# Hybrid mLSTM/MLA trunk: spilled feed-forward operands on ScalarE's DMA queue, loaded two chunks sooner; residuals a chunk later; context values in two parts

## The chip, the cores and the metric

One core of one Trainium2 chip runs the kernel. The metric is device microseconds (us) of one execution, the median over runs. TensorE (PE) multiplies, VectorE (DVE) and ScalarE (ACT) prepare and evacuate, GpSimd (POOL) and SyncE (SP) mostly issue DMAs; ACT can issue DMAs too.

## The reference, cut to what matters

Two layers over 256 latent and 256 context tokens of width 1024. Layer 0 mixes tokens with a chunked mLSTM, layer 1 with multi-head latent attention (MLA); each is followed by a gated convolutional feed-forward. The modulation rows ("ada") are a linear map of a condition vector.

```python
def _conv_ffn(h, w_in, conv_w, conv_b, w_out):
    gate, up = jnp.split(h @ w_in, 2, axis=-1)
    return (jax.nn.silu(_dwconv(gate, conv_w, conv_b)) * up) @ w_out
...
    m = jax.nn.silu(cond) @ w + b                       # _modulation: six parts per layer
...
    x = _layer_norm(ALPHA * x + ml[2] * yl, ln_g[i, 0], ln_b[i, 0])
    f = _conv_ffn(_modulate(x, ml[3], ml[4]), ffn_w_in[i], ffn_conv_w[i], ffn_conv_b[i], ffn_w_out[i])
    x = _layer_norm(ALPHA * x + ml[5] * f, ln_g[i, 1], ln_b[i, 1])
...
    kv = (_rms_norm(ckv, kv_norm) @ w_ukv).reshape(B, T, A_HEADS, A_DNOPE + A_DV)   # _mla_kv
    k_nope, v = jnp.split(kv, [A_DNOPE], axis=-1)
```

Context and latent tokens go through the same weights. All of it is float32 in and out.

## The kernel before, in words

**Products.** Every float32 product is three matmuls: each operand is split into a high and a low part, and `mm3` (L383 to L385) adds high by high, high by low and low by high. An operand's split is a copy on ACT and a subtraction on DVE; for weights that is L323 and L326.

**Weights.** `Stream` holds one list of weight pieces of 128x1024, in the order in which they are used. Its loads go out on SP's queue (L281), into a ring of raw buffers that depends on the stage; a load waits until the buffer's last split has ended. At most three split pieces (`w`, NB = 3) stand ready; pieces called wide go to other buffers (`wu`).

**Order.** Tile's planner places instructions on each engine's queue, mostly in the order in which the program names them. `keep_in_program_order` (`pin` in the code) fixes an instruction behind everything named before it on its engine. Background work is written as generators: `tick` runs a step of `bg` after each weight piece, and `n2` or an ADA number runs steps of `bg2`, which is the modulation (a step is one multiply-and-sum of 128x1024 on DVE, L512, and its rows come by SP's queue, L535). `ADA_M` is steps per piece of the mLSTM's output product, `ADA_F` steps per piece of the first feed-forward's input product.

**The feed-forward output of layer 0** (`w_fout0`) is a Strassen-like product of seven parts. The first four, in 24 chunks (`yt2`, `y11`, `yt3`, `yt1`, six of each), use operands that stay on the chip. The other three parts (`y21`, `y22`, `yt4`, six chunks each) use the operands named "2", "S4" and "3", which `act_sums` spilled to memory (`fd`, L1341 and L1347). `operand()` brings them back: it loads one (`zr`, L1367, one or two DMAs of 128 KB), and splits the one that was asked for two calls earlier (`fz`, L1373 on ACT, L1374 on DVE). There are 18 such operands. It is called at the chunks 10 to 23 and in the chunks of `y21` and `y22`. After chunk 23 the four products are copied out and added up (L1421 to L1433); then `residual()` forms the residual in eight background steps (L1441, L1442), and `add` puts the last products in (L1451 to L1453). The weights of `yt4` (and of its mLSTM sister `vt4`) are a sum: SP loads a piece that ACT spilled earlier (`raw<-t2d`, L278), and then POOL's queue adds the weights from memory into it (L279).

**After it** `mid` normalizes the context tokens, `mla_ctx` makes their compressed keys (`dkv`), `ukn(0)` the context keys (`kn`) and `uv(0)` the context values (`v`), while `tick`s run the latent tokens' normalization and transposes (`z_norm`, `ln_T`, L1199) in the background.

Of the kernel before, what the change touches and what calls it, by code (L numbers as in the profile page):

```python
# [38 lines left out]

VE = {1: (3, 0), 2: (3, 0), 3: (3, 0)}  # L40

ADA_U, ADA_T, ADA_Q, ADA_M, ADA_F = 1.4, 1.3, 1.6, 0.8, 1.05

# [309 lines left out]
class K:  # L355
# [996 lines left out]
    def w_fout0(self, x1d, mid):  # L1352


        nc, st, A = self.nc, self.st, self.fa
        pin = self.tc.keep_in_program_order
        parts = [("2", i) for i in range(6)] + [("S4", i) for i in range(6)] + [("3", i) for i in range(6)]
        off = {"2": 0, "3": 256, "S4": 512}
        got = []

        def operand():
            if parts:
                x, i = parts.pop(0)
                r = self.s2("zr")
                js = [j for j in (2 * i, 2 * i + 1) if j < 11]
                for h, j in enumerate(js):
                    pin(nc.gpsimd.dma_start(r[:, h * 256:(h + 1) * 256], self.fd[j][:, off[x]:off[x] + 256]))  # L1367
                got.append((x, js, r))
            if len(got) > 2 or not parts and got:
                x, js, r = got.pop(0)  # L1370
                n = 256 * len(js)
                u = self.u("fz")
                pin(nc.scalar.copy(u[:, 0, :n], r[:, :n]))  # L1373
                nc.vector.tensor_sub(u[:, 1, :n], r[:, :n], u[:, 0, :n])  # L1374
                for h, j in enumerate(js):
                    A[x, j] = u[:, :, h * 256:(h + 1) * 256]

        def prod(ps, x, w, i, bs=(0, 1)):
            for h in range(2 if i < 5 else 1):
                j = 2 * i + h  # L1380
                a = A[x, j]
                for b in bs:
                    ts = slice(b * 128, (b + 1) * 128)
                    cs = slice(h * 512, (h + 1) * 512)
                    self.mm3(ps[b], (a[:, 0, ts], a[:, 1, ts]), (w[0][:, cs], w[1][:, cs]), j == 0, j == 10)

        def pair():
            return [self.ps("y") for _ in range(2)]

        lo, hi = slice(0, 512), slice(512, 1024)  # L1390
        p6, p1, p7, p5 = [pair() for _ in range(4)]
        n = 0
        for i in range(6):
            for name, ps, x in (("yt2", p6, "S2"), ("y11", p1, "1"), ("yt3", p7, "S3"), ("yt1", p5, "S1")):
                w = st.use((name, 0, i))
                prod(ps, x, w, i)
                for f in ("S2", "1", "S3", "S1"):
                    if f == x:
                        for j in (2 * i, 2 * i + 1):
                            A.pop((f, j), None)  # L1400
                self.tick(1)
                if n >= 10:
                    operand()
                if n == 14:
                    gate = []
                    for g in (1, 0):
                        t = self.uf("gate")
                        nc.gpsimd.dma_start(t, self.gd[0, 5][g:g + 1, :].to_broadcast([128, 1024]))
                        gate.append(t)
                if n >= 16 and n % 2 == 0:  # L1410
                    if n == 16:
                        z = []
                    t = self.uf("z")
                    nc.gpsimd.dma_start(t, x1d[len(z)])
                    z.append(t)
                n += 1
        stats = [self.tiny(12, "st").rearrange("p (a b) -> p a b", b=6) for _ in range(4)]
        u1, u3, u4, vv = [], [], [], []
        for b in range(2):
            u = self.s2("u1")  # L1420
            nc.scalar.copy(u, p1[b])  # L1421
            u1.append(u)
            u = self.s2("u2")
            nc.vector.tensor_tensor(u, p6[b], u1[b], op=ALU.add)
            u4.append(u)
        for b in range(2):
            u = self.s2("u3")
            nc.vector.tensor_tensor(u, p7[b], u4[b], op=ALU.add)
            u3.append(u)
        for b in range(2):  # L1430
            v = self.s2("v")
            nc.vector.tensor_tensor(v, p5[b], u3[b], op=ALU.subtract)
            nc.vector.tensor_tensor(u4[b], p5[b], u4[b], op=ALU.subtract)  # L1433
            vv.append(v)

        def residual():

            for us, g, c in ((u1, 0, lo), (u4, 0, hi), (u3, 1, lo), (vv, 1, hi)):
                for b in range(2):
                    zz = z[2 * g + b]  # L1440
                    nc.vector.tensor_tensor(us[b], us[b], gate[g][:, c], op=ALU.mult)  # L1441
                    nc.vector.scalar_tensor_tensor(zz[:, c], zz[:, c], ALPHA, us[b], op0=ALU.mult, op1=ALU.add)  # L1442
                    if us is vv:
                        nc.vector.bn_stats(stats[2 * g + b][:, 1], zz[:, c])
                    yield

        def add(g, c, ps):
            for b in range(2):
                t = self.s2("zp")
                zz = z[2 * g + b][:, c]  # L1450
                nc.vector.tensor_tensor(t, ps[b], gate[g][:, c], op=ALU.mult)  # L1451
                nc.vector.tensor_tensor(zz, zz, t, op=ALU.add)
                nc.vector.bn_stats(stats[2 * g + b][:, c.start // 512], zz)  # L1453

        self.bg.append(residual())
        ps = pair()
        for i in range(6):
            w = st.use(("y21", 0, i))
            prod(ps, "2", w, i)
            self.tick(1)  # L1460
            operand()
        add(0, lo, ps)
        ps = pair()
        for i in range(6):
            w = st.use(("y22", 0, i))
            prod(ps, "S4", w, i)
            self.tick(1)
            operand()
        self.drain()
        add(0, hi, ps)  # L1470
        self.bg = [mid(0, z[0:2], stats[0:2])]
        self.step(self.bg)
        ps = pair()
        for i in range(6 - YTAIL):
            w = st.use(("yt4", 0, i))
            prod(ps, "3", w, i)
            self.tick(2)
        self.drain()
        mid(None, None, None)
        ws = [(i, st.use(("yt4", 0, i), hold=True)) for i in range(6 - YTAIL, 6)]  # L1480
        for b in range(2):
            for i, w in ws:
                prod(ps, "3", w, i, (b,))
        st.unhold("yt4")
        self.fa = self.fd = None
        self.bg = [mid(1, z[2:4], stats[2:4], lambda: add(1, lo, ps))]
# [94 lines left out]
            u = self.kn[h]  # L1581
            self.split(u[:, 0, cs], u[:, 1, cs], ps[:, hs])

    def uv(self, g):
        for t in (2 * g, 2 * g + 1):
            ts = slice(t * 128, (t + 1) * 128)
            for h in range(2):
                ps = self.ps("v1")
                c = slice(h * 512, (h + 1) * 512)
                for k in range(2):  # L1590
                    self.mm3(ps, (self.ckT[k][:, 0, ts], self.ckT[k][:, 1, ts]),
                             (self.wv[k][0][:, c], self.wv[k][1][:, c]), k == 0, k == 1)
                u = self.u("v1")
                self.split(u[:, 0], u[:, 1], ps)
                self.v1.append(u)
# [23 lines left out]
    def mla(self, hl):  # L1619
        nc, st = self.nc, self.st  # L1620
# [6 lines left out]
        for c in range(4):  # L1627
            w = st.use(("dq", 0, c))
            self.tick()
            for kk in range(2):  # L1630
                k = 2 * c + kk
                hi, lo = hl(k)
                cs = slice(kk * 384, (kk + 1) * 384)
                for t in range(2):
                    ts = slice(t * 128, (t + 1) * 128)
                    self.mm3(pss[t][:, :384], (hi[:, ts], lo[:, ts]), (w[0][:, cs], w[1][:, cs]), k == 0, k == 7)
        cq = []
        for t in range(2):
            r = self.s2("cq")
# [4 lines left out]
        g = self.smc("qng")  # L1644
# [11 lines left out]
        for c in range(2):  # L1656
            w = st.use(("uqr", 0, c))
            for kk in range(2 - c):
                k = 2 * c + kk
                cs = slice(kk * 512, (kk + 1) * 512)  # L1660
                for t in range(2):
                    ts = slice(t * 128, (t + 1) * 128)
                    self.mm3(pss[t], (cqT[k][:, 0, ts], cqT[k][:, 1, ts]), (w[0][:, cs], w[1][:, cs]),
                             k == 0, k == 2)
        self.drain()
        self.uv(1)
        self.ckT = self.wk = self.wv = None
        kn, v = self.kn, self.v1
        scale = float((DN + DR) ** -0.5)
# [2 lines left out]
        for t in range(2):  # L1672
            r = self.s2("qr")
# [111 lines left out]
def build(tc, off, a, out):  # L1785
    es = ExitStack()
    with es:
        k = K(tc, es, off, a)
        nc = k.nc
# [115 lines left out]
        st.pump(kv0 + PC)  # L1905
        k.mla_kv()
        k.ukn(0)
        k.tick(4)
        k.uv(0)
        k.drain()  # L1910
        k.take_late()
        att = k.mla(hl)
# [56 lines left out]
```

## Time and profile before

| what | value |
|---|---|
| median of 3 runs | 1399.56 us (1398.95 to 1405.11) |
| the profiled execution, its own time | 1403.48 us |
| its span, first to last instruction | 1401.7 us |
| mean granted TensorE clock | 0.992 |
| DMA queues, share of the 16 engines' span | SP's 48.1%, POOL's 13.9%, ACT's 3.0% |

The stages that the change touches: the mLSTM's output product ends at about 700 us of the span, the first feed-forward's input product runs from 720 to 946 us, `w_fout0`'s 24 chunks from 946 to 1007 us, `y21`, `y22` and `yt4` follow, and the context keys and values come from 1078 to 1097 us. Idle time of an engine is shown with the instruction after it and with what released that one. A window row gives, for each engine, busy us and the number of instructions, and then the granted clock, the DMA share and GB/s.

### The profile page before, as it was taken

The numbers are of one execution on the slowest core, as the hardware profiler recorded it, in microseconds if no ns is written. First come the engines' busy times: TensorE is split into PE (matmuls) and PEld (weight loads), VectorE is DVE, ScalarE is ACT, GpSimd is POOL, SyncE is SP. The second block draws the span as 40 slices with busy tenths as digits, with TensorE's granted clock in tenths as the row PEclk, the third lists the DMA queues.
The fourth block names the chain that finished last, engine by engine and source line by source line (L and its number), as shares of the span: only waits on it lengthen the run. The fifth ranks groups of instructions, "written<-read, shape, count | busy, mean of one in ns | idle before, by whom it ended". The sixth has DMA issues, their size and how long they took to land.

```text
span 1401.7 us, 19170 instructions
## 1 busy us (share of the span) xinstructions
PE 1359.0 (97%) x6903; PEld 1142.3 (81%) x6903; DVE 1074.7 (77%) x1726; ACT 699.5 (50%) x1179; POOL 139.0 (10%) x248
## 2 busy tenths in 40 slices
PE   6999999999999999999999999999968999999997
PEld 3788888888788888878798888888757988899986
DVE  6598756687688697699789777758878889776773
ACT  6585444435544545375543433434527667455560
POOL 0032000011011001110011000004111001000000
PEclk9999999999999999999999999999989999999999
DMA  9689847788675374667838667648767425367750
GB/s 336 222 293 321 282 163 240 244 293 283 203 226 194 102 243 152 210 214 229 255 134 289 221 224 213 213 146 292 263 174 223 148 83 202 122 190 229 206 189 30
DMA packets 94735, 297.63 MB, mean 212 GB/s; under 512 B 12136, under 2 KB 20584, under 8 KB 94640
## 3 DMA queue, kind: packets, MB, share of 16 engines
q1 hardware_dynamic: 68672, 218.52, 48.1%
q0 software_dynamic: 19056, 61.90, 13.9%
q10 hardware_dynamic: 6912, 15.99, 3.0%
q8 instruction: 54, 0.88, 0.2%
q14 instruction: 41, 0.34, 0.1%
HBM read 262.90 MB, written 33.46 MB: 211 GB/s over the span
## 4 chain that ended last, share of the span: by engine, by line
PE 44%; DVE 4%; DMA 3%; ACT 1%; issue 1%; POOL 0%; DVEq 0%; ACTq 0%; POOLq 0%; SPq 0%
PE fin L383 9%; PE fin L384 9%; PE fin L385 9%; PE y L384 4%; PE y L385 4%; PE y L383 4%; DMA raw<-in_ws 2%; DVE w L326 1%; DVE wu L326 1%; DMA zr<-fd 1%; PE s L1721 0%; DMA raw<-t2d 0%; PE dkv L383 0%; PE dkv L385 0%; PE dkv L384 0%
## 5 line engine op out<-in xcount | busy, mean ns | idle before, releaser
L326 DVE TENSOR_TENSOR w<-raw,w 128x1024 fp32r<-128x1024 f32 (+3 forms) x290 | 348.2, 1203 | 165.7 <-ACT w L323 165.0
L323 ACT CAST w<-raw 128x1024 fp32r<-128x1024 f32 (+3 forms) x290 | 300.4, 1037 | 331.1 <-PE fin L385 89.2
L384 PE MATMUL fin<-h,w 128*128 128x256 f32 (+1 forms) x696 | 231.7, 333 | 0.0
L385 PE MATMUL fin<-h,w 128*128 128x256 f32 (+1 forms) x696 | 231.4, 333 | 0.0
L383 PE MATMUL fin<-h,w 128*128 128x256 f32 (+1 forms) x696 | 231.2, 333 | 0.1
L512 DVE SCALAR_TENSOR_TENSOR junk<-ar,bc 128x1024 f32<-128x1024 f32 x128 | 155.8, 1217 | 3.6 <-ACT bc L554 1.7
L384 PEld LDWEIGHTS fin<-h,w 128*128 128x128 f32 x696 | 132.2, 190 | 13.1 <-DVE h L1212 0.2
L385 PEld LDWEIGHTS fin<-h,w 128*128 128x128 f32 x696 | 132.2, 190 | 12.7
L383 PEld LDWEIGHTS fin<-h,w 128*128 128x128 f32 x696 | 131.9, 190 | 13.1 <-ACT h L1211 0.3
L383 PE MATMUL qk<-xc,w 128*128 128x512 f32 x256 | 100.7, 393 | 0.0
L385 PE MATMUL qk<-xc,w 128*128 128x512 f32 x256 | 99.9, 390 | 0.0
L384 PE MATMUL qk<-xc,w 128*128 128x512 f32 x256 | 99.8, 390 | 0.0
L383 PEld LDWEIGHTS qk<-xc,w 128*128 128x128 f32 x256 | 48.1, 188 | 10.1 <-issue 0.4
L385 PEld LDWEIGHTS qk<-xc,w 128*128 128x128 f32 x256 | 48.1, 188 | 10.0
L384 PEld LDWEIGHTS qk<-xc,w 128*128 128x128 f32 x256 | 48.1, 188 | 9.6
L383 PE MATMUL up<-hT,w 128*128 128x512 f32 x128 | 50.5, 394 | 0.5 <-ACT hT L388 0.5
L384 PE MATMUL up<-hT,w 128*128 128x512 f32 x128 | 50.1, 392 | 0.5 <-DVE hT L389 0.5
L385 PE MATMUL up<-hT,w 128*128 128x512 f32 x128 | 50.1, 391 | 0.3 <-DVE w L389 0.3
L383 PE MATMUL tok<-w,hT 128*128 128x512 f32 x128 | 49.8, 389 | 0.0
L384 PE MATMUL tok<-w,hT 128*128 128x512 f32 x128 | 49.8, 389 | 0.0
L385 PE MATMUL tok<-w,hT 128*128 128x512 f32 x128 | 49.8, 389 | 0.0
L675 ACT ACTIVATE fg<-fg 128x512 f32<-128x512 f32 (+1 forms) x44 | 23.0, 523 | 53.6 <-DVE fg L673 48.0
(454 smaller groups left out, 3075.6 us busy)
## 6 DMA issues: line engine op xcount, KB each, us to landing
raw<-in_ws SPq DMA_DIRECT2D x287, 512.0 KB, 4.2
ar<-in_adaT SPq DMA_DIRECT2D x80, 512.0 KB, 4.4
adaw<-in_ada_w SPq DMA_DIRECT2D x32, 256.0 KB, 6.6
t2d<-raw ACTq DMA_DIRECT2D x13, 512.0 KB, 5.7
raw<-t2d SPq DMA_DIRECT2D x13, 512.0 KB
raw<-in_ws POOLq DMA_DIRECT2D x13, 512.0 KB, 7.7
zr<-fd POOLq DMA_DIRECT2D x33, 128.0 KB, 6.0
xmd<-xr POOLq DMA_DIRECT2D x16, 256.0 KB, 4.8
```

The source lines that it names most:

```text
L323: k.nc.scalar.copy(h[:, :cols], src)
L326: k.nc.vector.tensor_sub(l[:, :cols], src, h[:, :cols])
L383: mm(out, w[0], x[0], start=start, stop=False)
L384: mm(out, w[0], x[1], start=False, stop=False)
L385: mm(out, w[1], x[0], start=False, stop=stop)
L512: nc.vector.scalar_tensor_tensor(o, w, 1.0, self.bc[j], op0=ALU.mult, op1=ALU.mult, accum_out=col[:, k, j:j + 1])
L675: nc.scalar.activation(tmp[:, :n], tmp[:, :n], AF.Silu)
```

## The change: where operands are loaded, when, and what is paced

- `operand()` loads `zr` with `nc.scalar.dma_start` where it had `nc.gpsimd.dma_start`; it stays pinned, now on ACT.
- `operand()` is called from chunk 8 on, where it was chunk 10.
- `residual()` joins the background after the second chunk of `y21`, before its `tick`, where it joined ahead of the first.
- `uv` takes a list of token tiles; context tile 0's values are named ahead of `tick(4)`, tile 1's behind it.
- `ADA_M` goes from 0.8 to 0.6 and `ADA_F` from 1.05 to 1.25.

```diff
-ADA_U, ADA_T, ADA_Q, ADA_M, ADA_F = 1.4, 1.3, 1.6, 0.8, 1.05
+ADA_U, ADA_T, ADA_Q, ADA_M, ADA_F = 1.4, 1.3, 1.6, 0.6, 1.25
...
-                    pin(nc.gpsimd.dma_start(r[:, h * 256:(h + 1) * 256], self.fd[j][:, off[x]:off[x] + 256]))
+                    pin(nc.scalar.dma_start(r[:, h * 256:(h + 1) * 256], self.fd[j][:, off[x]:off[x] + 256]))
...
-                if n >= 10:
+                if n >= 8:
                     operand()
...
-        self.bg.append(residual())
         ps = pair()
         for i in range(6):
             w = st.use(("y21", 0, i))
             prod(ps, "2", w, i)
+            if i == 1:
+                self.bg.append(residual())
             self.tick(1)
             operand()
...
-    def uv(self, g):
-        for t in (2 * g, 2 * g + 1):
+    def uv(self, ts):
+        for t in ts:
...
-        self.uv(1)
+        self.uv((2, 3))
...
         k.ukn(0)
+        k.uv((0,))
         k.tick(4)
-        k.uv(0)
+        k.uv((1,))
         k.drain()
```

## The prediction, made before the change was run

> **What bounds the kernel now.** I read the page's busy times first, then windows of 5 us, then the chain of waits, then each engine's instructions in order of time at the one wide hole.
>
> ```profile
> PE 1359.0 (97%) x6903; PEld 1142.3 (81%) x6903; DVE 1074.7 (77%) x1726; ACT 699.5 (50%) x1179; POOL 139.0 (10%) x248
> ```
>
> TensorE is busy for 1359.0 of 1401.7 us, so all its waits together are 42.7 us, and a change that removes no matmul can win only from those. One hole is a quarter of them (columns: stretch, its us, busy us of PE, PEld, DVE, ACT, POOL with instructions, granted clock, DMA share, GB/s):
>
> ```profile
> 1030.00:1035.00 5.00, 1.05 (x5) 0.54 (x3) 0.00 (x0) 0.00 (x0) 0.31 (x1) 0.95 1.01 262
> 1035.00:1040.00 5.00, 0.00 (x0) 0.00 (x0) 3.27 (x6) 1.87 (x3) 0.88 (x1) 0.50 0.80 143
> ```
>
> From 1030 to 1035 us PE, DVE and ACT all stand while the DMA engines are full. The chain of waits (start, us, what) says for whom:
>
> ```profile
> 1019.93 5.27 DMA raw<-t2d
> ...
> 1025.77 0.90 POOL raw L279
> 1026.67 0.23 POOL zr L1367
> 1026.90 9.11 DMA zr<-fd
> ...
> 1040.15 1.14 DVE w L326
> ```
>
> POOL's adding DMA (L279) waits for a spilled weight; the last three operand loads stand behind it on POOL's queue, go out at 1026.7 and take 9.11 us. ACT's half of the operand's split waits for them, DVE's half for ACT's, and the weight split that PE wants stands behind that in DVE's order:
>
> ```profile
> 1036.73 1.03 DVE L1374 TENSOR_TENSOR fz<-zr,fz 128x512 fp32r<-128x512 f32 x2 [7.34 <-ACT fz L1373]
> ```
>
> ```profile
> 1041.34 0.80 PE L384 MATMUL y<-w,fz 128*128 128x512 f32 x1 [10.29 <-DVE w L326]
> ...
> 1043.64 0.63 PE L384 MATMUL y<-w,fz 128*128 128x512 f32 x1
> 1044.07 0.63 PE L385 MATMUL y<-w,fz 128*128 128x512 f32 x1
> ...
> 1045.09 0.39 PE L385 MATMUL y<-w,fz 128*128 128x512 f32 x1
> 1045.31 0.39 PE L383 MATMUL y<-w,fz 128*128 128x512 f32 x1
> ```
>
> The operands waited for are "3", used only in `yt4`, after the six pieces of `y22`: the order of the queues makes this stall, not need. PE starts the third piece of `y22` 10.29 us late, and then runs at a step of 0.43 instead of 0.22 us up to about 1044.9, some 1.5 us more.
>
> **The change part by part.**
>
> *The wait removed.* Calls from chunk 8 on issue 16 of the 18 loads ahead of `y21`; the last split is named in `y21`'s fourth piece, and no load stands behind L279 any more. DVE's 7.34 us of idleness goes. But DVE is full ahead of the hole:
>
> ```profile
> 1014.53 0.69 DVE L1374 TENSOR_TENSOR fz<-zr,fz 128x512 fp32r<-128x512 f32 x1
> 1015.14 0.69 DVE L1442 SCALAR_TENSOR_TENSOR z<-z,u 128x512 f32<-128x512 f32 x1
> 1015.74 1.22 DVE L326 TENSOR_TENSOR w<-raw,w 128x1024 fp32r<-128x1024 f32 x1
> ```
>
> ```profile
> 1007.07 0.50 PE L383 MATMUL y<-w,fz 128*128 128x512 f32 x1 [0.68 <-ACT u L1421]
> ...
> 1017.02 0.50 PE L384 MATMUL y<-w,fz 128*128 128x512 f32 x1 [1.02 <-DVE w L326]
> ```
>
> Instructions of 512 columns follow each other every 0.6 us, and at 1017.02 PE waited for DVE alone. Two operand splits move out of this stretch into the 24 chunks ahead: 2 x 0.6 = 1.2 us. One residual step (L1441 and L1442, 1.2 us) comes behind the split of `y22`'s third piece instead of ahead of it. That piece is ready 7.34 + 1.2 + 1.2 = 9.7 us earlier, at 1031.6; PE had run dry at 1041.34 - 10.29 = 1031.05, so about 1 us of waiting stays: DVE is late next. The late step is given back within `y22`, so DVE's last split there gains 7.34 + 1.2 = 8.5; PE's slow matmuls, 1.5 us, lay behind that and mostly go. Together 10.0 us. Bounds: 7.3, DVE's hole alone, and 12.8, all of 10.29 + 1.02 + 1.5.
>
> Does the short rest that stays slow the clock? These did:
>
> ```profile
> 690.79 0.50 PE L384 MATMUL y<-wu,hn 128*128 128x512 f32 x1 [0.57 <-DVE wu L326]
> ...
> 692.20 0.49 PE L383 MATMUL y<-wu,hn 128*128 128x512 f32 x1 [0.68 <-ACT wu L323]
> ...
> 693.45 0.80 PE L384 MATMUL y<-wu,hn 128*128 128x512 f32 x1 [0.76 <-DVE wu L326]
> 694.04 0.63 PE L385 MATMUL y<-wu,hn 128*128 128x512 f32 x1
> ```
>
> 2.0 us in three pieces, and a slow matmul of 0.63 us behind them; the one 1.02 us at 1017.02 had 0.50 and no more. I count nothing, bound 1.5. The Trainium skill, "TensorE: Matmul & The Clock Gate", Part 1 on the HAM clock gate, lets the half clock come after an idle window of some 3.4 us. By that a rest of 1 us costs nothing, and the sum stays; by the row at 693.45 it could be 1.5 us worse, since there 2.0 us were enough.
>
> *The new wait.* 33 DMA issues leave POOL's queue for ACT's. The mLSTM already does this with loads of its own:
>
> ```profile
> raw<-in_ws POOLq DMA_DIRECT2D x13, 512.0 KB, 7.7
> zr<-fd POOLq DMA_DIRECT2D x33, 128.0 KB, 6.0
> ...
> xcr<-xcd ACTq DMA_DIRECT2D x16, 256.0 KB, 8.4
> ```
>
> ```profile
> 331.62 0.85 ACTq L711 DMA_DIRECT2D xcr<-xcd  x2
> ...
> 339.29 0.62 ACT L716 CAST xc<-xcr 128x512 fp32r<-128x512 f32 x1 [1.17 <-DMA xcr<-xcd]
> ```
>
> ```profile
> DMA to landing us min/median/max: 2.2/6.0/10.1
> ```
>
> (KB each, median us to landing; then ACT in time; then the landing of `zr` on POOL.) Two issues take 0.85 us of ACT's queue. ACT rests longer than that per chunk:
>
> ```profile
> 992.83 1.06 ACT L323 CAST w<-raw 128x1024 fp32r<-128x1024 f32 x1 [1.10 <-PE y L385]
> ...
> 1000.99 0.62 ACT L323 CAST w<-raw 128x512 fp32r<-128x512 f32 x1 [1.52 <-PE y L385]
> ...
> 1004.67 0.61 ACT L1373 CAST fz<-zr 128x512 fp32r<-128x512 f32 x1
> ```
>
> What counts is landing. POOL ran far ahead of use; pinned on ACT, a load has its split two calls later. A chunk is 12 matmuls of 0.22, 2.7 us; two of them and one weight copy make 6.4 us, and the rest of 1.10 makes 7.5, under which a landing is hidden. The last four chunks are half as long: a load issued at 1000.99 has its split where 1004.67 stands, 3.7 us on. Behind that split on ACT are `y21`'s weight copies and the copies L1421, for which PE waits already at 1007.07. With the median of 6.0 they come 2.3 us late, with 2.2 not at all, with 10.1 6.4 us. I take 1.5 lost: nearest the median, less something for POOL's own queueing. The Trainium skill, "DMA: Bandwidth & Descriptors", section on issuing engines not being separate DMA queues, speaks against more: whoever issues, the same 16 engines carry it and only issue time is saved. By that the landing stays as it was and 2.3 is lost; the 9.11 us above agrees as far as a full DMA goes, but 1000 to 1010 us is not that stretch.
>
> *`yt4`'s weights.* PE comes 10 us earlier; do their sums?
>
> ```profile
> 1036.41 0.88 POOL L279 DMA_DIRECT2D raw<-in_ws  x1 [6.10 <-issue]
> ```
>
> ```profile
> 1051.63 0.69 DVE L1451 TENSOR_TENSOR zp<-y,gate 128x512 f32<-128x512 f32 x1 [1.05 <-PE y L385]
> ```
>
> The third lands at 1036.4 + 7.7 = 1044.1 if nothing moves it and is split 2.3 us later, at 1046.4; PE ended `y22` at 1051.6, so it wants that piece at 1051.6 - 10 + 2 x 2.7 = 1047. Hidden by 0.6 us; a landing of 10.1 costs 1.8. The later three wait for buffers that come free 8 to 10 us earlier. I take 0.5 lost, between 0 and 2.
>
> *Pacing.* 22 pieces carry `ADA_M`: 22 x 0.2 = 4.4 steps of L512 leave the mLSTM's output product for the feed-forward.
>
> ```profile
> L512 DVE SCALAR_TENSOR_TENSOR junk<-ar,bc 128x1024 f32<-128x1024 f32 x128 | 155.8, 1217 | 3.6 <-ACT bc L554 1.7
> ```
>
> ```profile
> 660.00:670.00 10.00, 10.00 (x49) 8.10 (x48) 10.00 (x20) 5.48 (x10) 0.55 (x1) 1.00 0.69 198
> 730.00:760.00 30.00, 30.00 (x134) 24.85 (x133) 29.23 (x49) 12.58 (x22) 6.51 (x12) 1.00 0.88 298
> ```
>
> That is 4.4 x 1.217 = 5.4 us of DVE, which is full at 660 to 670; its late weight splits free the buffers late, and the waits at 690 to 693 (2.0 us, then 1.4 us of slow matmuls) follow. Gain 0 to 3.4; I take 1.5. In the feed-forward PE never waits between 730 and 760, though DVE is at 29.23 of 30; 0.2 steps in each 5.4 us are 1.3 us more there, and two split pieces stand ready against it. Cost 0, up to 1.3 if they do not cover.
>
> *Context values in two parts.* Tile 0's 12 matmuls, 2.7 us, are named ahead of the transposes at which PE rests:
>
> ```profile
> 1083.72 0.78 PE L1199 MATMUL zT<-ident,z 128*128 128x128 f32 x4 [1.75 <-issue]
> 1085.27 0.39 PE L383 MATMUL kn<-ckT,wu 128*128 128x256 f32 x1 [0.77 <-DVE kn L389]
> ```
>
> ```profile
> 1083.66 1.16 DVE L326 TENSOR_TENSOR wu<-raw,wu 128x1024 fp32r<-128x1024 f32 x1
> ```
>
> But the second half of their weights is split only at 1084.8, so they fill little of 1.75 + 0.77 = 2.5 us, and could hold the transposes up by 1. I take 0.7 gained, from -1 to 2.5.
>
> **The sum.** 10.0 - 1.5 - 0.5 + 1.5 - 0 + 0.7 = 10.2 us. The profiled execution took 1403.48 us and would take 1393.3; it lies 3.9 above the median of the runs, which goes from 1399.56 to 1389.4.
>
> **The rivals.** *DVE and the sums keep half of it.* If the landing at the end of the chunks is 10.1 (6.4 lost instead of 1.5) or the slow clock and late sums cost 1.5 + 1.8, 4 to 5 us go: about 1394.5. For it speaks that DVE is full on both sides of the hole; against it that the hole itself is idle on every engine.
>
> *ACT becomes the bound: slower.* The load three calls on is named behind the split of this one, so three chunks can't be shorter than one landing and a split of 0.6 us. At 2.7 us a chunk this binds from a landing of 7.6 us; with 10.1 the chunk is 3.57 us, and 16 calls lose 14 us, which eats the gain: 1403. Slower by 0.5% needs 10.8 us; with 11.2, 19 us are lost, 1409. For it: `xcr` took 8.4 us on ACT's queue. Against: that wait at 339.29 was one of 1.17 us in 16 loads.
>
> *The change doesn't do what it says.* The planner could leave an unrelated wait in the same place on DVE, for instance ACT on `yt4`'s first sum: 1399.6.
>
> **How the numbers follow.** About 0.5% (7 us) is what a measurement of this kernel can tell from no change. Forecast, with its own range of 1386 to 1392.5: 0.56. Half of it, 1392.6 to 1398: 0.22. No change: 0.07. ACT's bound: 0.10, of which 0.03 ends within 0.5%. Better than 1386, where the upper bounds of pacing and values both come: 0.05. Faster by 0.5% is 0.56 + 0.05 = 0.61, the same 0.22 + 0.07 + 0.03 = 0.32, slower 0.07. The range leaves out ACT's bound and most of no change and of the better one: 1385 to 1398.5.
>
> **What would show it.** Right: no `zr` on POOL, no wait of DVE's L1374 near 7 us, PE's longest wait in `y22` under 2.5 us, `yt4` some 10 us earlier; fewer waits at 690; less rest at 1084. Wrong: ACT's L1373 waiting for `zr` by more than 2 us again and again, L1421 late, or ACT's L323 waiting for `yt4`'s sums.

## The result, and the profile after

The changed kernel takes 1388.92 us in the median of 4 runs (1388.60 to 1389.13), beside 1400.90 us (1398.95 to 1405.11, 4 runs) of the kernel before on the same chip: a ratio of 0.9910, 95% interval 0.9886 to 0.9935. Run again later it took 1387.91 us, 0.9904 (0.9890 to 0.9919). So it is faster, and about 12 us go. Its profiled execution took 1389.13 us with a span of 1387.4 us, 14.3 us under the profiled one of before; that one was among the slower of its kernel.

The page's busy line says that TensorE still does the same work:

```profile
PE 1355.8 (98%) x6903; PEld 1140.1 (82%) x6903; DVE 1075.0 (77%) x1726; ACT 699.2 (50%) x1179; POOL 121.2 (9%) x215
```

POOL issues 33 instructions fewer (215 for 248). The windows of 5 us in which the hole lay (columns as before) now look so; the same chunks come some 10 us earlier, so the window behind is shown too:

```profile
1025.00:1030.00 5.00, 3.65 (x17) 2.68 (x16) 5.00 (x8) 1.05 (x1) 0.38 (x2) 1.00 1.04 256
1030.00:1035.00 5.00, 5.00 (x24) 4.14 (x23) 5.00 (x8) 1.67 (x2) 0.83 (x1) 1.00 0.91 221
1035.00:1040.00 5.00, 5.00 (x24) 4.14 (x23) 5.00 (x8) 2.14 (x3) 0.00 (x0) 1.00 0.96 285
```

The DMA engines are as full as before, but VectorE no longer stands for them. It is busy for 5.00 of 5 us in each window: that is who is late next. TensorE's waits (line waited for: us in total, times, longest) and its rests in time:

```profile
PE y L384 <- DVE w L326: 3.2, 3, 1.3
...
PE y L383 <- ACT u L1421: 2.0, 1, 2.0
...
PE dkv L383 <- ACT hl L1211: 1.5, 1, 1.5
```

```profile
690.55 0.50 PE L384 MATMUL y<-wu,hn 128*128 128x512 f32 x1 [0.76 <-DVE wu L326]
...
1004.00 0.50 PE L383 MATMUL y<-w,fz 128*128 128x512 f32 x1 [2.04 <-ACT u L1421]
...
1010.89 0.50 PE L384 MATMUL y<-w,fz 128*128 128x512 f32 x1 [0.77 <-DVE w L326]
...
1027.72 0.50 PE L384 MATMUL y<-w,fz 128*128 128x512 f32 x1 [1.35 <-DVE w L326]
```

The row at 1027.72 is the third piece of `y22`, for which TensorE waited 10.29 us before. The one at 690.55 is all that is left of the three rests before 694. The loads, on the page:

```profile
zr<-fd ACTq DMA_DIRECT2D x33, 128.0 KB, 3.2
```

The 3.2 us there covers only 13 of the 33 loads, those whose landings the view could match. Read for every load from the events of its own semaphore in the trace, the landing takes 2.0 to 6.1 us, 4.0 in the median. For the kernel before, the view covers all 33: 2.2 to 10.1, and 6.0.

The first matmul of each stage, in each profiled execution, tells where the time went (us; "fin" is the first feed-forward's input product, "keys" the first matmul of `dkv`). The input product starts at 703.7 us in the kernel before, not at 720:

| kernel | start of fin | fin to `y21` | `y21` to keys | keys to end of span |
|---|---|---|---|---|
| before | 703.7 | 303.4 | 56.4 | 338.2 |
| changed | 699.3 | 304.7 | 44.6 | 338.8 |
| changed, run again | 698.0 | 304.6 | 44.7 | 338.9 |

So 4.4 us come ahead of the feed-forward, 1.3 are lost ahead of `y21`, 11.8 come from `y21` to `yt4`, and 0.6 are lost behind: 14.3 together.

### The profile page after: what moved, and what is told of

The parts are those of the page before. It is cut to its first block, busy times and chain, and to the rows that moved or that the text cites. A ratio compares the mean times of both kernels' runs of the same rounds, so it can differ in the third digit from the quotient of the medians.

```text
span 1387.4 us, 19172 instructions
## 1 busy us (share of the span) xinstructions
PE 1355.8 (98%) x6903; PEld 1140.1 (82%) x6903; DVE 1075.0 (77%) x1726; ACT 699.2 (50%) x1179; POOL 121.2 (9%) x215
## 3 DMA queue, kind: packets, MB, share of 16 engines
q1 hardware_dynamic: 68672, 218.52, 48.9%
## 4 chain that ended last, share of the span: by engine, by line
PE 86%; DVE 7%; DMA 3%; ACT 2%; issue 2%; ACTq 0%; SPq 0%; DVEq 0%
PE fin L383 9%; PE fin L384 9%; PE fin L385 9%; PE tok L383 6%; PE tok L385 6%; PE tok L384 6%; PE qk L383 4%; PE qk L384 4%; PE qk L385 4%; PE y L384 4%; PE y L385 4%; PE y L383 4%; PE up L383 2%; PE up L385 2%; PE up L384 2%
## 5 line engine op out<-in xcount | busy, mean ns | idle before, releaser
L326 DVE TENSOR_TENSOR w<-raw,w 128x1024 fp32r<-128x1024 f32 (+3 forms) x290 | 347.9, 1203 | 159.1 <-ACT w L323 158.3
L383 PEld LDWEIGHTS qk<-xc,w 128*128 128x128 f32 x256 | 48.1, 188 | 10.2 <-issue 0.4
L326 DVE TENSOR_TENSOR wu<-raw,wu 128x1024 fp32r<-128x1024 f32 (+1 forms) x33 | 39.1, 1200 | 8.2 <-ACT wu L323 7.9
```

Of the source, the lines that this page charges most:

```text
L326: k.nc.vector.tensor_sub(l[:, :cols], src, h[:, :cols])
L383: mm(out, w[0], x[0], start=start, stop=False)
```

## The experiments

Ratios are to the kernel before, run beside it on the same chip (its median was 1402.3, 1401.9 and 1401.8 us in the three groups), with 95% intervals.

### The queue alone

```diff
-pin(nc.gpsimd.dma_start(r[:, h * 256:(h + 1) * 256], ...   # operand(), kernel before
+pin(nc.scalar.dma_start(r[:, h * 256:(h + 1) * 256], ...
```

> The kernel before with the spilled operands on ScalarE's queue alone (calls still from chunk 10; residuals, values and pacing as before). Theory 'order': the stall of 10.3 us is made by three loads standing behind GpSimd's adding DMA, so the queue alone ends it: VectorE's longest wait at L1374 under 2 us, 6 to 9 us faster than before, less 1 to 2 us where the half chunks leave a load only 3.7 us. Rival 'late': the loads are simply asked for too late, so the same calls two chunks later than in the changed kernel still leave VectorE or ScalarE 3 us or more of waiting for zr in y21 or y22: under 5 us faster.

1397.15 us; 0.9964 (0.9950 to 0.9977), some 5 us: the theory's mechanism, and the low end of its gain. `y21` to keys is 48.9 us. No load stands behind an adding DMA any more and the hole goes: VectorE's longest wait at L1374 is 1.26 us. But TensorE still waits for VectorE at the third piece of `y22`, and the matmul there is a slow one:

```profile
1031.97 0.79 PE L384 MATMUL y<-w,fz 128*128 128x512 f32 x1 [3.21 <-DVE w L326]
```

Its wait for L1421 is 1.52 us, where it was 0.68.

### Two chunks sooner alone

```diff
-                if n >= 10:
+                if n >= 8:
                     operand()
```

> The kernel before with the operands asked for from chunk 8 on, still on GpSimd's queue. Then all 33 loads stand ahead of the first adding DMA on that queue. Theory 'order': as good as the other queue or better by 1 to 2 us, since ScalarE holds no loads: 7 to 10 us faster than before, TensorE's wait for L1421 under 1 us. Rival 'queue': a load on GpSimd's queue lands late whatever stands ahead of it (median 6.0 us before), so the wait of L1374 stays above 3 us and less than 5 us is won.

1394.47 us; 0.9944 (0.9926 to 0.9962), 7.8 us; `y21` to keys 45.8 us. POOL issues all 33 loads ahead of its first adding DMA, the last at 1003.88, so the queue need not change for the hole to go. The gain came as expected; a wait for L1421 under 1 us did not. ScalarE in time:

```profile
1004.35 1.05 ACT L323 CAST w<-raw 128x1024 fp32r<-128x1024 f32 x1 [0.43 <-PE y L385]
1005.30 0.62 ACT L1373 CAST fz<-zr 128x512 fp32r<-128x512 f32 x1
1005.82 1.05 ACT L323 CAST w<-raw 128x1024 fp32r<-128x1024 f32 x1
1006.77 0.61 ACT L1373 CAST fz<-zr 128x512 fp32r<-128x512 f32 x1
1007.29 1.04 ACT L323 CAST w<-raw 128x1024 fp32r<-128x1024 f32 x1
1008.23 0.58 ACT L1421 COPY u<-y 128x512 f32<-128x512 f32 x1
1008.71 0.62 ACT L1373 CAST fz<-zr 128x512 fp32r<-128x512 f32 x1
1009.23 0.58 ACT L1421 COPY u<-y 128x512 f32<-128x512 f32 x1
```

```profile
1008.86 0.50 PE L383 MATMUL y<-w,fz 128*128 128x512 f32 x1 [1.83 <-ACT u L1421]
```

No instruction there waits for a landing: ScalarE runs back to back. But since its last wait (1004.35) three weight copies and two splits stand ahead of the first L1421, which frees a product's buffer for `y21`; in the kernel before it was two of each, and TensorE waited 0.68 us.

### The pacing alone

```diff
-ADA_U, ADA_T, ADA_Q, ADA_M, ADA_F = 1.4, 1.3, 1.6, 0.8, 1.05
+ADA_U, ADA_T, ADA_Q, ADA_M, ADA_F = 1.4, 1.3, 1.6, 0.6, 1.25
```

> The kernel before with ADA_M 0.6 and ADA_F 1.25 alone. Theory: the 3.6 us by which the changed kernel is ahead at the first matmul of the feed-forward are all from pacing: first 'fin' matmul at 699 to 700 us instead of 703.7, 3 to 4 us faster than before; the hole at 1030 us stays, 10 us. Rival: the two traces differ there by chance of the landings, and pacing gives under 1.5 us.

1397.34 us; 0.9968 (0.9955 to 0.9981), 4.5 us by the ratio, a little over the 3 to 4 expected. fin starts at 698.8, `y21` to keys is 55.4 us, and the hole stays, if shorter (TensorE waits 7.99 us where it was 10.29), on ScalarE and on VectorE:

```profile
1028.90 0.62 ACT L1373 CAST fz<-zr 128x512 fp32r<-128x512 f32 x1 [4.81 <-DMA zr<-fd]
```

```profile
1029.55 1.03 DVE L1374 TENSOR_TENSOR fz<-zr,fz 128x512 fp32r<-128x512 f32 x2 [5.04 <-ACT fz L1373]
```

From fin to `y21` it takes 303.4 us, as before: the steps that move there cost nothing. Over all profiled executions fin starts at 700.4 to 704.3 with the old pacing (5 kernels) and at 698.0 to 699.3 with the new (9): 3.4 us on average.

### On ScalarE's queue, and four chunks later

Before with the loads on ScalarE's queue, called from chunk 14 on (`n >= 14`).

> The kernel before with the operands on ScalarE's queue and asked for four chunks later than before (from chunk 14 on), so that the last two operands are asked for in the first two pieces of y22, in the same full stretch where the three loads took 9.11 us. Theory 'order': they are not behind an adding DMA, land in 3 to 6 us, and no wait at L1374 is over 3 us; total within 3 us of the queue alone. Rival 'full DMA': whoever issues in that stretch waits 9 us, ScalarE waits 3 us or more for zr in y22, and the total is 3 to 8 us above the queue alone.

1396.76 us; 0.9965 (0.9948 to 0.9981): no worse than from chunk 10 on. ScalarE waits four times for a landing, 5.9 us in total. The longest wait, with the issues of the last loads (the split is that of the pair at 1024.71):

```profile
1024.71 1.11 ACTq L1367 DMA_DIRECT2D zr<-fd  x2
...
1025.88 0.69 ACTq L1367 DMA_DIRECT2D zr<-fd  x1
...
1031.71 0.62 ACT L1373 CAST fz<-zr 128x512 fp32r<-128x512 f32 x1 [3.02 <-DMA zr<-fd]
```

By their semaphores these three land after 6.0 to 6.6 us, with no adding DMA ahead of them on their queue; all 33 take 2.0 to 7.2, 4.1 in the median. So each side has a part. A stretch in which the DMA engines are full (a share of 1.01 from 1025 to 1032 us) makes a load slow and ScalarE wait 3 us even so, as the rival said. But the time is not above that of the queue alone and VectorE's longest wait at L1374 is 0.7 us, as the theory said: the split is named four calls later here, behind the weight split that TensorE wants.

### The changed kernel again, and with POOL's queue

The first is the changed kernel itself; the second has its `operand()` back on `nc.gpsimd`.

> The changed kernel once more, to stand beside the three others on one chip: 1388 to 1390 us.

> The changed kernel with the operands back on GpSimd's queue; everything else as changed, so asked for from chunk 8 on, with all 33 loads ahead of the first adding DMA. Theory 'sooner is enough': within 1.5 us of the changed kernel, the wait for L1421 still 1.8 to 2 us, since two more splits stand ahead of those copies on ScalarE, whatever queue carries the loads. Rival 'landing on ScalarE's queue costs' (the prediction's own term): the wait for L1421 falls to 0.7 us and the total to 1387 to 1388.

1387.91 us, 0.9904 (0.9890 to 0.9919), and 1388.32 us, 0.9906 (0.9891 to 0.9920). The first is just under its 1388 to 1390; the second is as "sooner is enough" had it. The queue, the first thing that the change names, is worth nothing measurable once the loads go out sooner. The wait for L1421 stays on POOL's queue too, where no split ahead of it waits for a load and the third weight copy stands ahead of it as above:

```profile
PE y L383 <- ACT u L1421: 1.8, 1, 1.8
```

### The changed kernel without the early context values

```diff
-        k.uv((0,))
         k.tick(4)
-        k.uv((1,))
+        k.uv((0, 1))
```

> The changed kernel with both parts of the context values behind the ticks, as before. Theory 'nothing': the 2 us of rest that the values fill ahead of the transposes come back at the latent keys (L1211), so the total stays within 0.7 us of the changed kernel; TensorE rests at 1068 to 1072 again and no longer for hl. Rival from the prediction: 0.7 us or more slower without it.

1388.83 us; 0.9912 (0.9897 to 0.9926). The interval overlaps that of the changed kernel, but beside it on the same chip the median is 0.9 us higher, and the four runs (1388.37 to 1389.90) lie just above the other's four (1387.72 to 1388.35). By its number that is nearer to the rival than to "nothing"; four runs each do not settle it. The rest at the transposes is back:

```profile
1068.62 1.09 PE L1199 MATMUL zT<-ident,z 128*128 128x128 f32 x4 [1.75 <-issue]
```

The latent tokens' keys start at 1082.3, 2.0 us later than in the changed kernel, and end at the same time. What happens in between, in the changed kernel (TensorE in time; then windows of 2 us):

```profile
1080.29 0.41 PE L383 MATMUL dkv<-w,hl 128*128 128x320 f32 x1 [1.51 <-ACT hl L1211]
...
1083.01 0.47 PE L384 MATMUL dkv<-w,hl 128*128 128x320 f32 x1
1083.28 0.47 PE L385 MATMUL dkv<-w,hl 128*128 128x320 f32 x1
...
1086.54 0.31 PE L385 MATMUL dkv<-w,hl 128*128 128x320 f32 x1
1086.68 0.31 PE L383 MATMUL dkv<-w,hl 128*128 128x320 f32 x1
```

```profile
1082.00:1084.00 2.00, 2.00 (x10) 2.00 (x9) 2.00 (x6) 1.36 (x4) 0.00 (x0) 0.55 0.00 0
1084.00:1086.00 2.00, 2.00 (x11) 2.00 (x10) 2.00 (x5) 0.83 (x1) 0.38 (x1) 0.60 0.00 0
```

The values fill the old rest, so TensorE comes to the latent tokens before their operand `hl` is made, rests 1.51 us, and then runs at a step of 0.27 instead of 0.147 us, with half the clock, from 1082.2 to 1085.6: that loses 3.4 x (1 - 0.147 / 0.27) = 1.5 us. Without the early values the clock is 1.00 in each of these windows; there it is halved earlier, from 1068.4 to 1075.2, behind the rest at the transposes. Nor is the loss at `hl` certain: the rest there is 1.50 to 1.51 us in all six profiled executions with early values, and the half clock follows in four. In the two where it does not (the changed kernel on POOL's queue, and the next run), keys to end of span takes 338.1 us, where the changed kernel takes 338.8 and 338.9.

### The two copies L1421 ahead of the splits

The changed kernel with both copies pinned on ScalarE at chunk 22.

```diff
+                if n == 22:
+                    for b in range(2):
+                        u = self.s2("u1")
+                        pin(nc.scalar.copy(u, p1[b]))
+                        u1.append(u)
                 if n >= 8:
                     operand()
...
-            u = self.s2("u1")
-            nc.scalar.copy(u, p1[b])
-            u1.append(u)
```

> The changed kernel with the two copies of the first product (L1421) named at chunk 22, two chunks ahead of the four products' end, instead of behind the last operand splits. Theory: TensorE's wait of 2.0 us ahead of y21 is those copies' place on ScalarE; it goes to under 0.4 us, and 0.5 to 2 us are won (1387 to 1388.5), not all, as VectorE is full from there to the end of y22. Rival: VectorE bounds that stretch throughout, so the wait returns at y22's third piece (1.35 us becomes 3) and nothing is won.

1388.08 us; 0.9908 (0.9891 to 0.9925). The wait for L1421 is gone, and stands in another line:

```profile
PE y L384 <- DVE w L326: 4.7, 3, 2.5
```

`y21` starts at 1001.3, and `y21` to keys takes 47.2 us instead of 44.6. One wait of 2.50 us stands in `y21`, with half the clock for 3.4 us behind it, and still the third piece of `y22` starts as far behind fin as before (329.1 us, for 328.5) and waits 1.17 us. So the rival was right: VectorE sets the end of this stretch, and TensorE's wait ahead of it had cost nothing.

### Loads on POOL's queue, two chunks later

Before with `n >= 12`.

> The kernel before with the spilled operands still on GpSimd's queue, but issued a chunk later (at chunk 12 instead of 10), so that more of them stand behind adding DMAs that wait for VectorE. Theory (the loads are late because of their place behind the adding DMAs): the wait of VectorE at L1374 for its landing grows or comes more than once, output tile 21 starts to finish 3 to 10 us later than in the kernel before, and the time is 1402 to 1411 us. Rival (they are late because of the load on the DMA engines at that time, whatever their place): the hole stays as it is, within 1 us of the kernel before, 1399 to 1403 us.

1402.24 us; 1.0008 (0.9996 to 1.0019). Both ranges hold this time, so it decides nothing; by mechanism each is half right. Seven loads instead of three stand behind adding DMAs, in three places, and ScalarE waits longer for them in total (9.6 us in 4 waits, against 7.1 us in one):

```profile
  ACT fz L1373: 9.6, 4
```

```profile
DMA to landing us min/median/max: 2.3/6.5/12.4
```

But the waits are spread, the longest is 3.41 us, and so the hole does not stay as it was. `y21` to keys takes 53.7 us, less than the 56.4 of before; the theory wanted `y21` to finish 3 to 10 us later. So the number of loads behind adding DMAs does not set the price; what sets it among several waits stays open. That the hole came from the place in the queue rests on the runs that left no load behind an adding DMA, and not on this one.

### Sooner on POOL's queue with the new pacing

The kernel before with `n >= 8` and the new `ADA_M` and `ADA_F`; queue, residuals and context values as before.

> The kernel before with the operands issued two chunks sooner on GpSimd's queue and with the two new pacing numbers; residuals and context values stay as they were. Theory (sooner and pacing make the gain and add up: 7.8 and 5.0 us by the runs of each alone): 12.5 to 13 us under the kernel before, 1388.5 to 1390 us. Rival (residuals a chunk later are needed, since without it VectorE holds output tiles 21 and 22 up again): no more than 10 us under the kernel before, 1391.5 us or more.

1389.36 us; 0.9921 (0.9906 to 0.9936), which is 12.5 us by the medians and 11.1 by the ratio. As the theory had it: two edits of the change make nearly all of it. The changed kernel, 0.9904 (0.9890 to 0.9919) and 0.9910 (0.9886 to 0.9935), is 0.4 to 1.5 us better in the median, and the intervals overlap. The residuals' edit was not run alone.

### Six residual multiplications on GpSimd

```diff
+            for us, g, c in ((u1, 0, lo), (u4, 0, hi), (u3, 1, lo)):   # residual(), first step
+                for b in range(2):
+                    nc.gpsimd.tensor_tensor(us[b], us[b], gate[g][:, c], op=ALU.mult)
...
-                    nc.vector.tensor_tensor(us[b], us[b], gate[g][:, c], op=ALU.mult)
+                    if us is vv:
+                        nc.vector.tensor_tensor(us[b], us[b], gate[g][:, c], op=ALU.mult)
```

> The changed kernel with six of the eight residual multiplications (L1441) on GpSimd instead of VectorE: six times 0.6 us less on VectorE, six times about 1.4 us more on GpSimd ahead of its adding DMAs. Theory (VectorE bounds output tiles 21 and 22): output tile 21 is 2 to 3.5 us shorter and the time 1 to 3 us under the changed kernel, 1385 to 1387 us. Rival (the stretch is bounded by TensorE and by what waits for GpSimd's adding DMAs, or VectorE slows beside GpSimd's work): within 0.7 us of the changed kernel or above it, 1387.3 us or more.

1389.09 us; 0.9911 (0.9894 to 0.9927): the rival, with VectorE slowed. GpSimd, and VectorE beside it:

```profile
1004.24 10.13 POOL L1440 TENSOR_TENSOR u<-u,gate 128x512 f32<-128x512 f32 x6 [28.79 <-DVE u L1424]
```

```profile
1008.90 0.68 DVE L1433 TENSOR_TENSOR u<-y,u 128x512 f32<-128x512 f32 x1
1009.50 2.02 DVE L326 TENSOR_TENSOR w<-raw,w 128x1024 fp32r<-128x1024 f32 x1
1011.44 1.79 DVE L1374 TENSOR_TENSOR fz<-zr,fz 128x512 fp32r<-128x512 f32 x1
1013.15 1.78 DVE L1446 SCALAR_TENSOR_TENSOR z<-z,u 128x512 f32<-128x512 f32 x1
1014.85 0.68 DVE L1374 TENSOR_TENSOR fz<-zr,fz 128x512 fp32r<-128x512 f32 x1
```

```profile
1016.72 0.50 PE L384 MATMUL y<-w,fz 128*128 128x512 f32 x1 [1.78 <-DVE w L326]
```

Three of VectorE's instructions take 0.80, 1.10 and 1.10 us longer than their like (1.22, 0.69 and 0.68): 3.0 us of the 6 x 0.6 = 3.6 that it was relieved of come back, and ahead of TensorE's second wait. The slowed ones read two operands from on-chip memory; L1433, with one operand from a product (`y`), keeps 0.68. The Trainium skill, "SBUF — State Buffer", section "SBUF: two separate sides", has a VectorE operation with two such inputs and a GpSimd operation lock each other out of a shared port for a whole instruction. These rows agree: the excess is up to 1.10 us, under one GpSimd instruction (10.13 / 6 = 1.69).

### The same, with the copies ahead

Both edits above together.

> The same six multiplications on GpSimd, and the two weight copies of L1421 ahead of the splits on ScalarE as well. Theory (with VectorE relieved, the boundary wait of 2.0 us that only moved before is now won): 0.5 to 1.5 us under the run with the multiplications alone, 1384 to 1386.5 us. Rival (VectorE still has too much to do): the wait shows again at L326, and the time is that of the run with the multiplications alone, within 0.5 us.

1391.96 us; 0.9936 (0.9922 to 0.9951). Both missed: it is 3 to 4 us slower than either edit alone. Four of VectorE's instructions are slowed between 1003.7 and 1015.5 (to 1.76 to 2.30 us), the first and second of them ahead of this wait of `y21`:

```profile
1011.65 0.80 PE L384 MATMUL y<-w,fz 128*128 128x512 f32 x1 [4.58 <-DVE w L326]
```

The clock is at 0.50 from 1010 to 1015 us. No version was found that beats the changed kernel.

## Why the prediction was right, and where its terms were not

The forecast was 1389.4 us, the measured median 1388.92. That the time is met to 0.5 us is luck. The gain is not met as closely: 10.2 us were forecast and 12.0 measured beside the kernel before, whose median there was 1.3 us above the one that the forecast started from, and 14.0 beside the later runs of it. What was right is the range, and the mechanism of the two large terms. In the two profiled executions the gain is 14.3, and by terms:

**The wait removed and the sums: 10.0 - 0.5, measured 11.8.** That is from `y21` to the keys. The path was as described: no operand load on POOL, no wait of VectorE's L1374 near 7 us, and the third piece of `y22` is still 1.35 us late for VectorE (forecast: about 1). TensorE's rests in `y21` and `y22` fall from 1.02 + 0.95 + 10.29 = 12.3 to 0.77 + 1.35 = 2.1 us, that is by 10.1, and the 1.5 us of slow matmuls go wholly. What the term left out is one more rest of the kernel before, in `y22`'s first piece, which is gone too:

```profile
1025.31 0.50 PE L384 MATMUL y<-w,fz 128*128 128x512 f32 x1 [0.95 <-DVE w L326]
```

And the term took off 1.2 us for the late residual step, as given back within `y22`, and 0.5 for the sums of `yt4`. Neither was paid: behind 1027.72 no product of `y22` or `yt4` waits, though ScalarE waits 2.1 us once (at 1038.91) for a sum. Run alone, two chunks sooner gave 7.8 us (5.3 to 10.4 by the interval) against 10.0 - 1.5 - 0.5 = 8.0.

**The new wait: -1.5, measured -1.3.** TensorE's wait for L1421 grows from 0.68 to 2.04 us, as the step said, by a late landing at the last split ahead of it:

```profile
1002.85 0.62 ACT L1373 CAST fz<-zr 128x512 fp32r<-128x512 f32 x1 [1.04 <-DMA zr<-fd]
1003.37 0.58 ACT L1421 COPY u<-y 128x512 f32<-128x512 f32 x1
```

That split's load took 4.4 us to land and no load more than 6.1, where the step went by a median of 6.0. (The 8.4 us of `xcr`, which spoke for ScalarE's bound, also covers a part of its loads: all 16 have a median of 5.4.) Two things it did not see: on POOL's queue, without a late landing, a third weight copy ahead of L1421 costs the same 1.8 us; and the wait is not a term of the sum at all, since with the copies ahead the time is the same. It belonged inside VectorE's.

**Pacing: 1.5, measured 4.4 in these two executions and 3.4 on average; the step that was mis-sized.** The mechanism is the one named: the rests at 690 to 694 fall from 2.0 to 0.8 us, and the slow stretch behind them is gone. Windows of before and then of after:

```profile
690.00:695.00 5.00, 2.99 (x8) 1.75 (x8) 3.12 (x5) 2.70 (x4) 0.00 (x0) 0.82 0.76 236
695.00:700.00 5.00, 5.00 (x20) 4.04 (x19) 4.34 (x6) 2.29 (x3) 0.00 (x0) 0.84 0.82 215
```

```profile
690.00:695.00 5.00, 4.45 (x20) 3.71 (x21) 3.71 (x6) 2.10 (x2) 0.00 (x0) 1.00 0.71 223
695.00:700.00 5.00, 5.00 (x27) 4.26 (x26) 4.38 (x7) 1.25 (x2) 0.00 (x0) 1.00 0.80 230
```

TensorE does 28 matmuls in these 10 us before and 47 after; some of the 47 belong to the next stage and are shorter. The forecast took under half of its own bound of 3.4, and the bound was short. It left out some 0.7 us that came ahead of 685 us (the last product of the ordinary pieces starts at 683.9 instead of 684.7, the first 0.1 earlier). And a rest costs more than its idle time: at the three rests TensorE took 0.97, 1.08 and 1.25 us from one matmul to the next, where the step is 0.23, so 2.6 us and not 2.0. The profiled execution of before also showed more of this loss than most of its kind: fin started at 703.7, and at 700.4 to 704.3 over the five with the old pacing. `ADA_F` cost nothing, as forecast.

**Context values: +0.7, not settled.** The stretch behind the keys takes 338.8 us instead of 338.2 in these two executions. The step said what could fill the rest, and not what TensorE would reach then: `hl` is late, and the rest of 1.5 us there halves the clock in four executions of six. Without this part the median is 0.9 us higher on one chip, and the intervals overlap (0.9912 and 0.9904 or 0.9910).

On the clock, for which nothing was counted: in the changed kernel the rests that stayed in `y21` and `y22` (0.77 and 1.35 us) did not slow it, nor did the one of 2.04 ahead of `y21`; the new one at `hl` did.

The rivals: ScalarE did not become the bound, since the longest landing was 6.1 us (7.2 when the kernel ran again) and it needed 7.6. "VectorE keeps half" did not come either, but its mechanism holds for what is left: VectorE is full from 1005 to 1040 us, and where a wait for ScalarE was taken away there, one for L326 came in its place.

## What to carry to other kernels

A load that is issued on a queue with waiting work is as late as that work: first see what stands ahead of it, and issue it sooner before changing the queue, since sooner alone removed the hole here. Where a view gives a landing time, see how many of the loads it covers. Price a removed rest with the slow clock behind it, and look up who is late at the place that the engine will reach instead. A wait just ahead of a stretch in which another engine is full may cost nothing: taken away here, it moved.

## What the runs showed of the hardware that was not expected

**The clock halves after short rests, but not after each.** By the granted clock in the traces, half-speed stretches between 600 and 1110 us last 3.41 us or two or three times that: 1082.2 to 1085.6 above, and 1006.4 to 1009.8 in the run with loads two chunks later on POOL's queue, after this rest:

```profile
1006.30 0.70 PE L383 MATMUL y<-w,fz 128*128 128x512 f32 x1 [1.84 <-ACT u L1421]
```

Rests of 1.51 and 1.84 us brought it on, and one of 2.04 us (at 1004.00 of the changed kernel) did not. Within one execution the slow stretches start whole multiples of 3.413 us apart (in the changed kernel on POOL's queue at 1003.96 and 1188.28 us, 54 of them). So the windows can be counted back, and TensorE's rest in each can be added up. Over the 14 profiled executions, from 600 to 1110 us, the windows at full clock divide so: with 1.80 us of rest or more half the clock followed each time (18 windows), with 1.4 us or less never, and with 1.60 to 1.79 us 7 times of 12. An edge of a window cuts the rest at `hl` in the two executions where the clock stayed, and it cuts the 2.04 us into 1.71 and 0.33. What decides between 1.60 and 1.79 us is not settled. The Trainium skill, "TensorE: Matmul & The Clock Gate", Part 1, gives free-running windows of some 3.4 us. The length and the spacing of the slow stretches agree; that an idle window has to pass first does not, since windows with about half of their time at rest were enough.

**An issue on ScalarE's queue can hold ScalarE.** One of these issues takes 0.33 to 0.57 us (32 of 33 in the changed kernel). A pair once held the queue for 3.86 us, with ScalarE's next split behind it:

```profile
988.41 3.86 ACTq L1367 DMA_DIRECT2D zr<-fd  x2
992.37 0.62 ACT L1373 CAST fz<-zr 128x512 fp32r<-128x512 f32 x1 [2.91 <-DMA raw<-in_ws]
```

The second issue of the pair took 0.32 us like the others, but it ran only at 991.95: it waited for the semaphore that is to tell of its landing. That semaphore was still in use for a weight load, which SP had issued at 987.16 and which landed at 991.93. So two loads of different queues that share a semaphore can hold each other up, and on ScalarE's queue that holds its computing too. TensorE had split pieces left and did not wait.
